# A hybrid decoder layer on one core: a new cost table for the order of the queues, an alternating first merge, attention blocks in twos

## The chip, the core and the metric

The kernel runs on one core of one Trainium2 chip. The core has a matrix engine (TensorE, PE in the profile; PEld is its loading of weights), a vector engine (VectorE, DVE), a scalar engine (ScalarE, ACT), a general engine (GpSimd, POOL) and a queue that issues transfers (SyncE, SP). Each engine works through its own instructions in the order in which the program holds them. The metric is the time of one execution in microseconds (us), as the median of several.

## The reference

One decoder layer in float32 on 1024 tokens of width 1024:

```
x = x + 0.5 * SwiGLU_1(rmsnorm(x))                 # 1024 -> 2816 -> 1024
h = rmsnorm(x);  columns = h @ w_in                # one projection for both branches
A: causal dilated window attention, 3 groups (dilations 1, 4, 16), 4 heads of 64 each, blocks of 128
B: gated DeltaNet, 8 heads of 128, chunks of 64, a triangular solve in each chunk
x = x + (sigmoid(g_a) * (A @ w_branch_a) + sigmoid(g_b) * (B @ w_branch_b)) @ w_out
x = x + 0.5 * SwiGLU_2(rmsnorm(x));  return rmsnorm(x)
```

## The kernel before

The program is one straight line: first feed-forward, mixer, merge of the branches, second feed-forward. Every large product is made of three float32r matmuls of 128 x 128 weights on 128 x 512 columns (high part, low part, cross part); `proj`, line 161, is the one of the mixer. They are called wide below.

Between them stand narrow matmuls in float32. `attention_pair` (lines 847 to 896) takes two heads of a group at a time and, for each of eight query blocks of 128, makes the scores of the two heads with 64 rows of weights each, one head in rows 0 to 63 of the array and one in rows 64 to 127 (L864, into two banks `tC`), masks them and takes the maximum on DVE (L867, L869), takes the exponential on ACT (L871), transposes on PE (L877, into `tM`), copies on DVE (L879), multiplies by the values on PE (L885, into `tA`), copies on ACT (L887) and stores (L896). `combine` (L910 to L931) reads the three groups back and weighs them, token tile by token tile.

`gdn_merge` joins the inverses of 32 x 32 blocks that `gdn_inverse_blocks` (L1036 to L1042, a long row of small DVE operations) has made: first in two quadrants of 32 rows (L1070 and L1075, eight chunks each, and one copy a quadrant), then in halves of 64 (L1083, L1090). In L1070 both quadrants write into one PSUM bank, on partitions 32 to 63 and 96 to 127.

The order on the engines doesn't follow the code. The program is built twice: `arrange` takes the first build, gives each instruction a cost (`Program.cost`) and a rank (the longest chain of costs from it to the end), and lets each engine in turn take the ready instruction of the highest rank; the second build is held to that order. `Program.turn` adds what PE loses between two kinds of matmul: R is wide, T a transpose, F a full float32 one, S the scores (64 rows), Q the small ones of the merge. A rule keeps PE on the instruction that follows in the code if its rank is at most `STAY` behind. Nothing of this runs on the chip; only the order that comes out does.

Of the kernel before, what the change touches and what calls it, by code (L numbers as in the profile page):

```python
# [8 lines left out]
F32 = mybir.dt.float32  # L9
F32R = mybir.dt.float32r  # L10
I32 = mybir.dt.int32
AF = mybir.ActivationFunctionType
# [3 lines left out]
P = 128  # L16
# [830 lines left out]
def attention_pair(C, w_in, g, hp, V):  # L847

    nc = C.nc
    q = rope_tile(C, w_in, C_QA + g * 256 + hp * P, g)  # L850
    k = rope_tile(C, w_in, C_KA + g * 256 + hp * P, g)
    with band(C, "att"):
        for b in range(NT):
            prev = (g == 0 and b > 0) or (g == 1 and b % 2 == 1)
            nk = 256 if prev else P
            mask = C.pair if g == 2 else (C.band if prev else C.band[:, P:])
            nj = nk // P
            o = C.at.tile([P, 132], F32, name="o", tag="o", bufs=3)
            nm = C.at.tile([P, 2], F32, name="nm", tag="nm", bufs=3)
            s = C.at.tile([P, 2, 256], F32, name="s", tag="s", bufs=3)  # L860
            ps = [psum(C, "tC") for _ in range(2)]
            for h in range(2):
                rows = slice(h * 64, h * 64 + 64)
                nc.tensor.matmul(ps[h][:, :nk], seq_tokens(q, rows, b), seq_tokens(k, rows, b, prev),  # L864
                                 start=True, stop=True)
            for h in range(2):
                nc.vector.tensor_tensor_reduce(s[:, h, :nk], ps[h][:, :nk], mask, 1.0, NEG, op0=ALU.add, op1=ALU.max,  # L867
                                               accum_out=o[:, 128 + h:129 + h])
            nc.vector.tensor_scalar(nm, o[:, 128:130], -0.125, None, op0=ALU.mult)  # L869
            for h in range(2):  # L870
                nc.scalar.activation(s[:, h, :nk], s[:, h, :nk], AF.Exp, bias=nm[:, h:h + 1], scale=0.125,  # L871
                                     accum_out=o[:, 130 + h:131 + h])
            pt = psum(C, "tM")
            for h in range(2):
                for j in range(nj):
                    c = (h * nj + j) * P
                    nc.tensor.transpose(pt[:, c:c + P], s[:, h, j * P:j * P + P], C.ident)  # L877
            pT = C.at.tile([P, 512], F32, name="pT", tag="pT", bufs=2)
            nc.vector.tensor_copy(pT[:, :2 * nk], pt[:, :2 * nk])  # L879
            po = psum(C, "tA")  # L880
            for h in range(2):
                for j in range(nj):
                    vb = b - 1 + j if prev else b
                    c = hp * P + h * 64
                    nc.tensor.matmul(po[:, h * 64:h * 64 + 64], pT[:, (h * nj + j) * P:(h * nj + j) * P + P],  # L885
                                     V[vb][:, c:c + 64], start=j == 0, stop=j == nj - 1)
            nc.scalar.copy(o[:, :P], po[:, :P])  # L887
            dst = C.od[g][:, hp, :]
            if g == 0:
                dst = dst[b * P:b * P + P, :]  # L890
            elif g == 1:
                r, n = b // 2, b % 2
                dst = dst.rearrange("(i r) f -> r i f", r=4)[r, n * P:n * P + P, :]
            else:
                dst = dst.rearrange("(i r) f -> r i f", r=8)[b]
            nc.sync.dma_start(dst, o)  # L896


# [157 lines left out]
def gdn_merge(C, N, Tm, Um):  # L1056

    nc = C.nc

    def rows(ps, n):  # L1060
        return ps[:, :4 * n].rearrange("p (c t) -> p c t", t=n)

    half = (slice(0, 4), slice(4, 8))

    quads = [(slice(b, b + 32), slice(b + 32, b + 64)) for b in (0, 64)]
    ps = psum(C, "tM")
    W = C.gd.tile([P, NT, 32], F32, name="W", tag="W", bufs=2)
    for lo, hi in quads:
        for c in range(NT):
            nc.tensor.matmul(ps[hi, c * 32:c * 32 + 32], N[lo, c, hi], Tm[lo, c, lo], start=True, stop=True)  # L1070
        nc.vector.tensor_copy(W[hi], ps[hi, :256].rearrange("p (c t) -> p c t", t=32))
    ps = psum(C, "tM")
    for lo, hi in quads:
        for c in range(NT):
            nc.tensor.matmul(ps[hi, c * 32:c * 32 + 32], Um[hi, c, hi], W[hi, c, :], start=True, stop=True)  # L1075
# [442 lines left out]
class Program:  # L1518
# [118 lines left out]
    def form(self, i):  # L1637
        aps = [a for a in i["ins"] if a["kind"] == "physical_ap"]
        if i["engine"] == "PE":
            if aps[0]["dtype"] == "float32r":  # L1640
                return "R"
            if i.get("is_transpose"):
                return "T"
            return "F" if aps[0]["ap"][0][1] > 64 else "S" if i["outs"][0]["ap"][0][1] > 64 else "Q"
        if i["engine"] == "Activation":
            return {"Exp": "E", "Silu": "U", "Sigmoid": "G", "Ln": "L"}.get(str(i.get("func")).split(".")[-1], "")
        return ""

    def turn(self, a, b, n):

        if a == b:
            return 0
        if b == "S" or b == "Q" or a == "Q":
            return (200 if n < 256 else 300) if a == "S" else 93
        if a == "S":
            return 200 if n < 256 else 300
        return -80 if b == "R" and a in "TF" else 6

    def run(self, a):
        n = 1  # L1660
# [6 lines left out]
    def cost(self, k):  # L1667
# [13 lines left out]
            n *= c  # L1681
        q = self.queue[k]
        if q == 0:
            t = {"R": n / 2.4 + 13, "T": 109, "F": 223, "S": 7, "Q": 117 if n > 32 else 63}[self.kind[k]]
            return t, t + 190 + (300 if self.kind[k] == "S" else 0)
        ps = any(self.place[a["memref"]][0] == "PSUM" for a in aps)
        if q == 1:
            t = 150 + 1.04 * n
# [18 lines left out]
STAY = 1000  # L1707


def hop(a, b):  # L1710
# [3 lines left out]
def arrange(prog, pools):  # L1714
# [15 lines left out]
    while stack:  # L1730
        k = stack.pop()
        rank[k] = cost[k][1] if k < n else 0.0
        for c, whole in kids[k]:
            rank[k] = max(rank[k], rank[c] + (cost[k][1] + hop(p.queue[k], p.queue[c]) if whole else 0))
# [21 lines left out]
    while count < n:  # L1756
# [19 lines left out]
        k = now[q][0][1]  # L1776
        if q == 0 and last[0] is not None:
            f = follow.get(last[0])
            if f is not None and not taken[f] and not left[f] and ready[f] <= t and rank[f] >= rank[k] - STAY:
# [14 lines left out]
        clock[q] = t + cost[k][0]  # L1794
        if q == 0:
            free0 = clock[q]
            clock[q] -= 80 if p.kind[k] in "TF" else 0
        end = t + cost[k][1]
        if p.dma[k]:
            end += max(0.0, wire - clock[q] - 1500)  # L1800
# [67 lines left out]
```

## Time and profile before

| | |
|---|---|
| median of 3 runs | 2573.09 us (2571.34 to 2573.66) |
| the profiled execution, its own time | 2572.86 us |
| its span in the trace | 2571.1 us |
| time outside the span | 1.8 us |
| instructions | 34921 |

A row of the timeline has the start in us, the busy time in us, engine, line, operation, the tiles written and read, and how many equal ones were merged into it. A float32 matmul that is no transpose runs as two passes and has two records: x16 at L1070 is eight matmuls. A row of the stages has the length of the stretch, the busy time of each engine with its instructions, the share of the TensorE clock that was granted, and the DMA share. A matmul's record is longer than its turn on PE, so what one costs is read from start to start. A row of waits has the waiting group, what it waited for, us in all, times, and the longest.

### The profile page before, as it was taken

To read this page: it belongs to the slowest core of one execution; us is meant where nothing else is said; L and a number is where in the kernel's file an instruction comes from. 1 tells how busy PE (TensorE), PEld (TensorE's weight loads), DVE (VectorE), ACT (ScalarE), POOL (GpSimd) and SP (SyncE) were. 2 spreads that over 40 slices of the span, in tenths; PEclk is the share of its full clock that TensorE was granted. 3 is DMA by queue.
4 is the path that set the end of the run, shared out by engine and by line. 5 is a ranking of instruction groups with operands and counts; after the bars stand their busy time and mean duration, and the time that the engine had idled before them with its cause. 6 is when DMAs were issued, how large, how long until landed. Compare 5 with 4: busy or idle time off the path is not lost.

```text
span 2571.1 us, 34921 instructions
## 1 busy us (share of the span) xinstructions
PE 2508.9 (98%) x12739; PEld 2074.0 (81%) x12739; DVE 1825.5 (71%) x4059; ACT 983.8 (38%) x1899; POOL 24.4 (1%) x36
## 2 busy tenths in 40 slices
PE   7999999999999999899999999989999999999996
PEld 7788888888888877688888888868888888888885
DVE  8867666768744455888888888546668766667578
ACT  4422332444422336333443335254443333333443
POOL 0000000000000000000000000000000000000000
PEclk9999999999999999999999999999999999999998
DMA  4233224836343331322222213255542223328453
GB/s 159 80 115 114 99 96 168 289 109 203 118 123 94 93 82 52 91 66 64 56 62 56 68 48 81 66 184 193 182 137 91 106 91 115 115 98 301 138 168 111
DMA packets 258172, 301.06 MB, mean 117 GB/s; under 512 B 41840, under 2 KB 175184, under 8 KB 258000
## 3 DMA queue, kind: packets, MB, share of 16 engines
q1 hardware_dynamic: 255696, 292.54, 34.8%
q10 hardware_dynamic: 2304, 6.29, 1.0%
q8 instruction: 100, 1.64, 0.3%
q14 instruction: 72, 0.59, 0.1%
HBM read 217.34 MB, written 75.14 MB: 114 GB/s over the span
## 4 chain that ended last, share of the span: by engine, by line
PE 90%; DVE 6%; DMA 2%; ACT 1%; issue 1%; SPq 0%; DVEq 0%; ACTq 0%
PE mm L161 22%; PE tC L404 13%; PE mm L404 8%; PE tM L404 8%; PE mm L584 4%; PE tC L584 4%; PE tA L161 3%; PE tM L584 3%; PE tA L584 3%; PE mm L697 2%; PE mm L274 2%; PE tC L274 2%; PE tC L1381 2%; PE mm L1381 2%; DMA sgl<-sgbd 1%; PE tA L885 1%
## 5 line engine op out<-in xcount | busy, mean ns | idle before, releaser
L216 ACT CAST fH<-fraw 128x512 fp32r<-128x512 f32 x482 | 289.1, 620 | 463.6 <-PE tM L404 89.4
L217 DVE TENSOR_TENSOR fL<-fraw,fH 128x512 fp32r<-128x512 f32 x482 | 323.0, 689 | 123.8 <-ACT fH L216 118.9
L161 PE MATMUL mm<-hH,fH 128*128 128x512 f32 x896 | 361.5, 410 | 8.7 <-ACT xp L955 5.0
L161 PE MATMUL mm<-hH,fL 128*128 128x512 f32 x896 | 361.0, 405 | 0.0
L161 PE MATMUL mm<-hL,fH 128*128 128x512 f32 x896 | 360.3, 404 | 0.0
L161 PEld LDWEIGHTS mm<-hH,fH 128*128 128x128 f32 x896 | 169.9, 190 | 43.4 <-ACT xp L955 6.2
L161 PEld LDWEIGHTS mm<-hH,fL 128*128 128x128 f32 x896 | 169.7, 190 | 33.3 <-issue 2.3
L161 PEld LDWEIGHTS mm<-hL,fH 128*128 128x128 f32 x896 | 170.1, 190 | 30.3 <-issue 1.7
L404 PE MATMUL mm<-hL,fH 128*128 128x512 f32 x320 | 124.5, 389 | 0.0
L404 PE MATMUL mm<-hH,fL 128*128 128x512 f32 x320 | 121.2, 389 | 0.1
L404 PE MATMUL mm<-hH,fH 128*128 128x512 f32 x320 | 119.0, 389 | 0.0
L576 ACT CAST fH<-hid 128x512 fp32r<-128x512 f32 x154 | 95.0, 617 | 53.1 <-DMA hid<-hd1x 15.8
L577 DVE TENSOR_TENSOR hid<-hid,fH 128x512 fp32r<-128x512 f32 x154 | 104.5, 685 | 5.5 <-ACT fH L576 5.5
L438 DVE TENSOR_TENSOR e<-tM,e 128x512 f32<-128x512 f32 x40 | 26.1, 687 | 79.0 <-PE tM L404 79.0
L216 ACT CAST fH<-hH 128x512 fp32r<-128x512 f32 x68 | 42.3, 622 | 91.3 <-PE tC L584 33.3
L867 DVE CUSTOM_DVE_ANT_0 s<-tC,masks 128x128 f32<-128x128 f32 (+1 forms) x96 | 30.4, 350 | 58.4 <-PE tC L864 35.1
L404 PEld LDWEIGHTS mm<-hH,fL 128*128 128x128 f32 x320 | 60.1, 188 | 13.0 <-DVE fL L217 0.5
L965 DVE SCALAR_TENSOR_TENSOR ka<-xp,cw,ka 128x512 f32<-128x512 f32 x96 | 69.4, 757 | 1.3 <-ACT ka L963 0.8
L404 PEld LDWEIGHTS mm<-hH,fH 128*128 128x128 f32 x320 | 60.0, 188 | 12.6 <-ACT e L408 0.2
L404 PEld LDWEIGHTS mm<-hL,fH 128*128 128x128 f32 x320 | 60.1, 188 | 12.4
L584 PE MATMUL tC<-fH 128*128 128x512 f32 x176 | 68.4, 390 | 0.0
L584 PE MATMUL tC<-fL,fH 128*128 128x512 f32 x176 | 68.2, 389 | 0.0
(402 smaller groups left out, 6200.4 us busy)
## 6 DMA issues: line engine op xcount, KB each, us to landing
fraw<-in_w_in_dram SPq DMA_DIRECT2D x66, 512.0 KB, 3.8
fraw<-in_ffn_w_gate_dram SPq DMA_DIRECT2D x22, 1024.0 KB, 5.2
fraw<-in_ffn_w_up_dram SPq DMA_DIRECT2D x22, 1024.0 KB, 7.2
hL<-in_ffn_w_down_dram SPq DMA_DIRECT2D x8, 1024.0 KB, 6.3
fraw<-in_ffn_w_down_dram SPq DMA_DIRECT2D x8, 1024.0 KB, 6.1
fraw<-in_w_branch_b_dram SPq DMA_DIRECT2D x8, 1024.0 KB, 5.6
fraw<-in_w_out_dram SPq DMA_DIRECT2D x8, 1024.0 KB, 7.3
vb<-xp ACTq DMA_DIRECT2D x48, 128.0 KB, 2.4
```

The costliest lines, as they stand in the source:

```text
L161: nc.tensor.matmul(ps, w, x, start=k == 0 and i == 0, stop=k == kt - 1 and i == 2)
L216: nc.scalar.copy(h, src)
L217: nc.vector.tensor_tensor(out=l, in0=src, in1=h.bitcast(F32), op=ALU.subtract)
L274: nc.tensor.matmul(ps[:, n0:n0 + n], w, x[:, k, c], start=k == 0 and i == 0, stop=k == KT - 1 and i == 2)
L404: nc.tensor.matmul(ps, w, x, start=opens and k == 0 and q == 0, stop=k == 3 and q == 2, skip_group_check=True)
L576: C.nc.scalar.copy(h, v.bitcast(F32))
L577: C.nc.vector.tensor_tensor(out=v, in0=v.bitcast(F32), in1=h.bitcast(F32), op=ALU.subtract)
L584: self.C.nc.tensor.matmul(ps, x[:, m], w, start=p == 0 and i == 0, stop=p == NPAIR - 1 and i == 2)
L697: nc.tensor.matmul(ps[:, :n], h[:, k, b * P:b * P + P], W[k][w], start=k == 0 and i == 0, stop=k == KT - 1 and i == 2)
L867: nc.vector.tensor_tensor_reduce(s[:, h, :nk], ps[h][:, :nk], mask, 1.0, NEG, op0=ALU.add, op1=ALU.max, accum_out=o[:, 128 + h:129 + h])
L965: nc.vector.scalar_tensor_tensor(o, x, w, o, op0=ALU.mult, op1=ALU.add)
L1381: nc.tensor.matmul(ps, mx[:, c], W[k][w], start=i == 0, stop=i == len(seq) - 1)
```

## The change

Three things are edited.

`attention_pair` handles query blocks b and b + 1 together. Their four score matmuls are written in one piece (head 0 and head 1 of the first block, then of the second), into the two halves of the same two `tC` banks; one operation scales the four maxima, one ACT copy takes both results out of `tA` and one transfer stores them: 24 of each in place of 48. The transposes, the copies of `pT` and the products with the values stay one for each block. The tiles `o`, `nm` and `s` are twice as large with two buffers in place of three.

`gdn_merge` issues its first two stages with the chunk as the outer loop, so that the two quadrants alternate, and copies both quadrants after all sixteen.

The table of `arrange` is new. PE's turns have other prices, and the two heads' scores are told apart as S and s; scores cost 106 + 0.83 ns a column. DVE and ACT are free for the next instruction 82 and 100 ns before the end of one, and an instruction that needs the result of the one just before on the same engine comes 40 ns after its end. While PE is on narrow matmuls it prefers a ready narrow one of a rank at most `LINGER` = 3000 behind; while on wide ones, a wide one at most `STAY` = 1000 behind.

```diff
-        for b in range(NT):
+        for b0 in range(0, NT, 2):
...
+            for i, (b, prev, nj, _) in enumerate(blocks):
+                for h in range(2):
+                    rows = slice(h * 64, h * 64 + 64)
+                    nc.tensor.matmul(ps[h][:, i * 256:i * 256 + nj * P], seq_tokens(q, rows, b), seq_tokens(k, rows, b, prev),
+                                     start=True, stop=True)
...
+            nc.scalar.copy(o[:, :, :P], po[:, :256].rearrange("p (b f) -> p b f", f=P))
...
+    for c in range(NT):
+        for lo, hi in quads:
+            nc.tensor.matmul(ps[hi, c * 32:c * 32 + 32], N[lo, c, hi], Tm[lo, c, lo], start=True, stop=True)
     for lo, hi in quads:
-        for c in range(NT):
-            nc.tensor.matmul(ps[hi, c * 32:c * 32 + 32], N[lo, c, hi], Tm[lo, c, lo], start=True, stop=True)
         nc.vector.tensor_copy(W[hi], ps[hi, :256].rearrange("p (c t) -> p c t", t=32))
...
-        if a == b:
+        if a == b or a + b == "Ss":
             return 0
...
+        t = (205 if n < 256 else 305) if a == "S" else 260 if b == "s" else 0
+        if b in "SsQ":
+            return t + (0 if a in "Ss" else 93)
...
-        return t, t
+        return t - (0, 82, 100, 0)[q], t
...
+            wide = p.kind[last[0]] == "R"
...
+            if f is not None and rank[f] >= rank[k] - (STAY if wide else LINGER):
                 k = f
...
-                at = clock[q]
+                at = end + 40 if q in (1, 2) else clock[q]
```

The instructions are the same 11692 matmuls; their order differs nearly everywhere. Counted over the whole order of PE, in unbroken stretches of one kind:

| stretches | before | changed |
|---|---|---|
| scores, of one / two / four matmuls | 16 / 40 / 0 | 2 / 9 / 19 |
| small ones of the merge (32 and 64 wide) | 76 | 56 |
| wide followed by a transpose or a full float32 one | 380 | 259 |
| neighbours in the 32-wide merge that lie in different rows of the array | 15 | 230 |

PE late in the attention, before (`s` are the exponentials, `ka` holds keys, queries or values):

```order
L885 MATMUL tA<-ka,pT 128x64 x2
L161 MATMUL mm<-hH_5387,fH 128x512
L161 MATMUL mm<-hL_5389,fH 128x512
L161 MATMUL mm<-hH_5387,fL 128x512
L864 MATMUL tC<-ka 128x128
L161 MATMUL mm<-hL_5719,fH 128x512
L161 MATMUL mm<-hH_5717,fL 128x512
L864 MATMUL tC<-ka 128x128
```

And in the changed program, where the lines of the same operations are 883, 866 and 890:

```order
L890 MATMUL tA<-ka,pT 128x64 x2
L883 MATMUL tM<-ident,s 128x128 x2
L890 MATMUL tA<-ka,pT 128x64 x2
L883 MATMUL tM<-ident,s 128x128 x2
L866 MATMUL tC<-ka 128x128 x4
L890 MATMUL tA<-ka,pT 128x64 x4
L161 MATMUL mm<-hH_5387,fH 128x512
```

Narrow matmuls stand together and the four scores of two blocks follow each other, where two heads of one block stood with wide ones between them.

PE at the first merge of head 0, before (`Tm`, `U` are the inverse and its transpose, `W` the first product):

```order
L1070 MATMUL tM<-Tm,ka 32x32 x4
L1075 MATMUL tM<-W,U 32x32 x8
L1070 MATMUL tM<-Tm,ka 32x32 x4
L161 MATMUL mm<-hH_5388,fL 128x512
L161 MATMUL mm<-hH_5388,fH 128x512
L161 MATMUL mm<-hL_5390,fH 128x512
L161 MATMUL mm<-hH_5388,fL 128x512
L1004 MATMUL tA<-seg,strictR 128x512 x2
L161 MATMUL mm<-hL_5720,fH 128x512
L161 MATMUL mm<-hH_5718,fL 128x512
L1075 MATMUL tM<-W,U 32x32 x4
```

And changed:

```order
L1074 MATMUL tM<-Tm,ka 32x32 x16
L161 MATMUL mm<-hH_5717,fH 128x512
L161 MATMUL mm<-hL_5719,fH 128x512
L161 MATMUL mm<-hH_5717,fL 128x512
L1080 MATMUL tM<-W,U 32x32
L161 MATMUL mm<-hH_5388,fL 128x512
L1080 MATMUL tM<-W,U 32x32 x15
```

The sixteen of a stage stand in one piece, and in it the two quadrants alternate.

DVE where `combine` (L910 to L925) meets the inverse of head 0 (L1036, L1037), before:

```order
L914 TENSOR_TENSOR cz<-ce,oc 128x12
L915 TENSOR_TENSOR cM<-cz 128x4
L916 TENSOR_TENSOR cM<-cM,cz 128x4
L917 RECIPROCAL cM<-cM 128x4
L918 TENSOR_TENSOR ce<-ce,cM 128x12
L922 TENSOR_TENSOR oc<-oc,ce 128x3x128 x2
L924 TENSOR_TENSOR cy<-oc 128x256
L925 TENSOR_TENSOR cy<-cy,oc 128x256
```

And changed (`combine` now at L914 to L929, the inverse at L1045 and L1046):

```order
L918 TENSOR_TENSOR cz<-ce,oc 128x12
L1045 TENSOR_TENSOR fsP<-fsT,Tm 128x80
L919 TENSOR_TENSOR cM<-cz 128x4
L217 TENSOR_TENSOR fL<-fraw,fH 128x512
L920 TENSOR_TENSOR cM<-cM,cz 128x4
L1046 TENSOR_REDUCE fsT<-fsP 128x4
L921 RECIPROCAL cM<-cM 128x4
L217 TENSOR_TENSOR fL<-fraw,fH 128x512
L1045 TENSOR_TENSOR fsP<-fsT,Tm 128x84
L922 TENSOR_TENSOR ce<-ce,cM 128x12
```

An instruction no longer stands right behind the one whose result it reads. From the first operation of `combine` to the first copy of the merge, DVE has 223 instructions before, of which 134 are read by their successor, and 252 in the changed program, of which 22 are; the 29 more are parts of head 1 (its convolutions, splits and sums). PE has 248 wide ones of `proj` from its last product of the attention to the first L1070 before, and 259 to the first L1074 in the changed program; the last product of the attention itself stands 72 wide ones earlier in the mixer.

More of the change, by code (lines that the diff above doesn't have):

```diff
@@ L852, in attention_pair @@
     with band(C, "att"):
-        for b in range(NT):
[L854 to L860, printed above, removed]
-            ps = [psum(C, "tC") for _ in range(2)]
[L862 to L879, printed above, removed]
-            po = psum(C, "tA")
[L881 to L887, printed above, removed]
@@ new lines, in attention_pair @@
+        for b0 in range(0, NT, 2):
+            blocks = []
+            for b in (b0, b0 + 1):
+                prev = (g == 0 and b > 0) or (g == 1 and b % 2 == 1)
+                mask = C.pair if g == 2 else (C.band if prev else C.band[:, P:])
+                blocks.append((b, prev, 2 if prev else 1, mask))
+            o = C.at.tile([P, 2, 132], F32, name="o", tag="o", bufs=2)
+            nm = C.at.tile([P, 2, 2], F32, name="nm", tag="nm", bufs=2)
+            s = C.at.tile([P, 2, 2, 256], F32, name="s", tag="s", bufs=2)
+            ps = [psum(C, "tC") for _ in range(2)]
+            for i, (b, prev, nj, _) in enumerate(blocks):
[3 more added lines that the diff above has]
+                                     start=True, stop=True)
+            for i, (b, prev, nj, mask) in enumerate(blocks):
+                for h in range(2):
+                    nc.vector.tensor_tensor_reduce(s[:, i, h, :nj * P], ps[h][:, i * 256:i * 256 + nj * P], mask, 1.0, NEG,
+                                                   op0=ALU.add, op1=ALU.max, accum_out=o[:, i, 128 + h:129 + h])
+            nc.vector.tensor_scalar(nm, o[:, :, 128:130], -0.125, None, op0=ALU.mult)
+            po = psum(C, "tA")
+            for i, (b, prev, nj, _) in enumerate(blocks):
+                for h in range(2):
+                    nc.scalar.activation(s[:, i, h, :nj * P], s[:, i, h, :nj * P], AF.Exp, bias=nm[:, i, h:h + 1], scale=0.125,
+                                         accum_out=o[:, i, 130 + h:131 + h])
+            for i, (b, prev, nj, _) in enumerate(blocks):
+                pt = psum(C, "tM")
+                for h in range(2):
+                    for j in range(nj):
+                        c = (h * nj + j) * P
+                        nc.tensor.transpose(pt[:, c:c + P], s[:, i, h, j * P:j * P + P], C.ident)
+                pT = C.at.tile([P, 512], F32, name="pT", tag="pT", bufs=2)
+                nc.vector.tensor_copy(pT[:, :2 * nj * P], pt[:, :2 * nj * P])
+                for h in range(2):
+                    for j in range(nj):
+                        vb = b - 1 + j if prev else b
+                        c = hp * P + h * 64
+                        nc.tensor.matmul(po[:, i * P + h * 64:i * P + h * 64 + 64], pT[:, (h * nj + j) * P:(h * nj + j) * P + P],
+                                         V[vb][:, c:c + 64], start=j == 0, stop=j == nj - 1)
+            nc.scalar.copy(o[:, :, :P], po[:, :256].rearrange("p (b f) -> p b f", f=P))
@@ L1067, in gdn_merge @@
     W = C.gd.tile([P, NT, 32], F32, name="W", tag="W", bufs=2)
+    for c in range(NT):
+        for lo, hi in quads:
+            nc.tensor.matmul(ps[hi, c * 32:c * 32 + 32], N[lo, c, hi], Tm[lo, c, lo], start=True, stop=True)
     for lo, hi in quads:
-        for c in range(NT):
-            nc.tensor.matmul(ps[hi, c * 32:c * 32 + 32], N[lo, c, hi], Tm[lo, c, lo], start=True, stop=True)
         nc.vector.tensor_copy(W[hi], ps[hi, :256].rearrange("p (c t) -> p c t", t=32))
     ps = psum(C, "tM")
+    for c in range(NT):
+        for lo, hi in quads:
+            nc.tensor.matmul(ps[hi, c * 32:c * 32 + 32], Um[hi, c, hi], W[hi, c, :], start=True, stop=True)
     for lo, hi in quads:
-        for c in range(NT):
-            nc.tensor.matmul(ps[hi, c * 32:c * 32 + 32], Um[hi, c, hi], W[hi, c, :], start=True, stop=True)
         nc.vector.tensor_copy(Tm[hi, :, lo], ps[hi, :256].rearrange("p (c t) -> p c t", t=32))
@@ L1733, in arrange @@
         for c, whole in kids[k]:
-            rank[k] = max(rank[k], rank[c] + (cost[k][1] + hop(p.queue[k], p.queue[c]) if whole else 0))
+            if whole:
+                near = p.queue[k] == p.queue[c] and not p.dma[k]
+                step = cost[k][1] + (hop(p.queue[k], p.queue[c]) if not near else 40 if p.queue[k] in (1, 2) else 0)
+                rank[k] = max(rank[k], rank[c] + (cost[k][0] if near and not p.queue[k] else step))
+            else:
+                rank[k] = max(rank[k], rank[c])
         for d in list(full[k]) + list(after[k]):
@@ L1778, in arrange @@
             f = follow.get(last[0])
-            if f is not None and not taken[f] and not left[f] and ready[f] <= t and rank[f] >= rank[k] - STAY:
+            wide = p.kind[last[0]] == "R"
+            if f is None or taken[f] or left[f] or ready[f] > t:
+                f = None
+            if f is None or (p.kind[f] == "R") != wide:
+                alike = [(r, c) for r, c in now[0] if not taken[c] and (p.kind[c] == "R") == wide]
+                f = min(alike)[1] if alike else f
+            if f is not None and rank[f] >= rank[k] - (STAY if wide else LINGER):
                 k = f
```

23 lines of the change are left out of this document (10 added, 13 removed).

## The prediction

> **What bounds the kernel now.** I read the page first, then the stages, then what PE waited for, then the timeline where PE changes its kind of work.
>
> ```profile
> span 2571.1 us, 34921 instructions
> PE 2508.9 (98%) x12739; PEld 2074.0 (81%) x12739; DVE 1825.5 (71%) x4059; ACT 983.8 (38%) x1899; POOL 24.4 (1%) x36
> PE 90%; DVE 6%; DMA 2%; ACT 1%; issue 1%; SPq 0%; DVEq 0%; ACTq 0%
> ```
>
> PE has work in flight for 98% of the span and is 90% of the chain that ended last. So most of what PE is spared comes off the time, and the question is what it is spared. Three stages of the mixer:
>
> ```profile
> 740.00:1030.00 290.00, 290.00 (x1694) 234.81 (x1694) 140.88 (x382) 115.34 (x343) 2.89 (x4) 1.00 0.30 84
> 1030.00:1108.00 78.00, 67.77 (x328) 53.85 (x326) 67.43 (x225) 27.81 (x54) 0.57 (x2) 0.93 0.36 97
> 1108.00:1690.00 582.00, 580.01 (x3567) 479.41 (x3567) 475.43 (x1354) 227.22 (x447) 19.75 (x26) 1.00 0.23 65
> ```
>
> Attention (first row) and heads 1 to 7 (third) never let PE run dry, while DVE is busy 141 of 290 us and 475 of 582. Between them, where `combine` and head 0 meet, PE is busy 67.8 of 78 us, DVE 67.4, and the clock falls to 0.93. What PE waits for there:
>
> ```profile
> PE mm L161 <- ACT xp L955: 5.0, 2, 4.9
> PE tA L928 <- DVE cM L916: 2.6, 1, 2.6
> PE tA L928 <- DVE cy L925: 2.4, 2, 2.1
> ```
>
> ```profile
> 1074.71 0.79 PE L161 MATMUL mm<-hH,fH 128*128 128x512 f32 x1 [4.86 <-ACT xp L955]
> 1075.30 0.63 PE L161 MATMUL mm<-hL,fH 128*128 128x512 f32 x1
> 1075.73 0.63 PE L161 MATMUL mm<-hH,fL 128*128 128x512 f32 x1
> ...
> 1079.11 0.39 PE L161 MATMUL mm<-hL,fH 128*128 128x512 f32 x1
> 1079.34 0.40 PE L161 MATMUL mm<-hH,fL 128*128 128x512 f32 x1
> ```
>
> A wide matmul takes 0.23 us from start to start (1079.11 to 1079.34) and 0.43 after the wait (1075.30 to 1075.73). From 1074.71 to 1079.11 that costs 2.2 us over ten wide ones at 0.23. With the waits (2.6, 2.1 and 4.9) this place loses about 12 us.
>
> **The change, part by part.**
>
> *Turns of PE, scores.*
>
> ```profile
> 1017.75 0.40 PE L161 MATMUL mm<-hH,fH 128*128 128x512 f32 x1
> 1018.07 0.48 PE L864 MATMUL tC<-ka 64*128 64x128 f32 x2
> 1018.49 0.50 PE L161 MATMUL mm<-hH,fL 128*128 128x512 f32 x1
> 1018.83 0.40 PE L161 MATMUL mm<-hH,fH 128*128 128x512 f32 x1
> ...
> 1020.84 0.40 PE L161 MATMUL mm<-hH,fH 128*128 128x512 f32 x1
> 1021.17 0.49 PE L864 MATMUL tC<-ka 64*128 64x128 f32 x4
> 1021.59 0.50 PE L161 MATMUL mm<-hL,fH 128*128 128x512 f32 x1
> 1021.93 0.27 PE L877 MATMUL tM<-ident,s 128*128 128x128 f32 x1
> 1021.96 0.48 PE L161 MATMUL mm<-hL,fH 128*128 128x512 f32 x1
> 1022.27 0.40 PE L161 MATMUL mm<-hH,fL 128*128 128x512 f32 x1
> ```
>
> Two heads' scores in one piece stand 0.42 us (1021.17 to 1021.59), and one head's alone stands 0.42 too (1018.07 to 1018.49). With the two wide ones around it, the one takes 1.09 us (1020.84 to 1021.93) and the other 1.08 (1017.75 to 1018.83), 0.63 and 0.62 over two wide ones. Hence a turn into scores and back costs 0.63 - 0.42 = 0.21, and a pair torn apart 2 x 0.62 - 0.63 = 0.61 more. Before, 8 of the 48 pairs are torn (16 stretches of one); of the change, one is: 7 x 0.61 = 4.3 us. The other 47 pairs stand in 28 stretches, 19 of which hold two pairs; each of those saves one turn, 19 x 0.21 = 4.0. The first pair of such a stretch goes on into the second head to head, which no row shows; if that costs a full turn, the 4.0 is nothing. The rows nearest to it are those of two heads in one piece, so I take it whole. Sum 8.3, bounds 4.3 and 8.3 (wider score tiles would only raise it).
>
> *Turns of PE, merge.*
>
> ```profile
> 1105.64 0.49 PE L1154 MATMUL tA<-ident,vT 128*128 128x128 f32 x3
> 1106.07 0.69 PE L1070 MATMUL tM<-Tm,ka 32*32 32x32 f32 x16
> 1106.68 0.73 PE L1004 MATMUL tA<-seg,strictR 128*128 128x512 f32 x2
> 1107.25 0.27 PE L1154 MATMUL tA<-ident,vT 128*128 128x128 f32 x1
> ...
> 1108.30 0.21 PE L1075 MATMUL tM<-W,U 32*32 32x32 f32 x1
> 1108.33 0.19 PE L1070 MATMUL tM<-Tm,ka 32*32 32x32 f32 x1
> 1108.36 0.19 PE L1075 MATMUL tM<-W,U 32*32 32x32 f32 x1
> ...
> 1108.42 0.48 PE L1075 MATMUL tM<-W,U 32*32 32x32 f32 x10
> 1108.71 0.21 PE L1070 MATMUL tM<-Tm,ka 32*32 32x32 f32 x1
> ```
>
> From 1108.42 to 1108.71 nine or ten passes start in one quadrant: 0.032 us each, 0.063 for a matmul of two passes. The stretch of eight from 1105.64 to 1107.25 takes 1.61 us; without three transposes at 0.11 (below) and two wide ones, 0.82; the eight at 0.063 are 0.51, so a turn costs 0.31. The change has 56 stretches of these in place of 76: 20 x 0.31 = 6.2 us.
>
> *Turns, transposes and full float32.* A transpose and the wide one after it take 0.34 us (1021.93 to 1022.27), so a transpose costs 0.11, which is about its own work: these turns are worth some 0.01. 121 fewer of them are 1.2 us. Turns together: 8.3 + 6.2 + 1.2 = 15.7, at least 11.7.
>
> *The alternating merge.* Between 1108.30 and 1108.36 a pass of one quadrant and one of the other start every 0.03 us, each quadrant at its own pace: two run at once. They overlap for about four matmuls at each change. With 230 neighbours of 240 in different quadrants, a matmul comes every 0.032 in place of 0.063: 230 x 0.031 = 7.1 us, less the 15 changes at 0.09 that exist, 1.4: 5.7 us. But there the two quadrants write different banks (L1070 and L1075 each have their own `tM`), and in the change they write the same one. No row shows this; the bounds are 5.7 and, if they take turns at 0.063, a loss of the 1.4. I take 5.7, since they lie on different partitions, as in the overlapping rows. That both copies now come after sixteen adds at most 8 x 0.063 = 0.5 us to a chain, which wide work hides.
>
> The Trainium skill speaks against this term: "TensorEngine Tiling (Array Packing)", Restrictions and Gotchas, says that different row tiles cannot access the same PSUM bank at the same time. By it the term would be a loss of 1.4 us and the time 7.1 us longer than mine.
>
> *DVE at `combine`.*
>
> ```profile
> 1034.19 0.17 DVE L918 TENSOR_TENSOR ce<-ce,cM 128x12 f32<-128x12 f32 x1
> 1034.28 0.68 DVE L979 TENSOR_REDUCE gssq<-sq 128x4 f32<-128x512 f32 x1
> ...
> 1036.73 0.17 DVE L125 TENSOR_SCALAR rgy<-rgv 128x16 int32<-128x16 int32 x1
> 1036.94 0.17 DVE L126 CUSTOM_DVE_ANT_0 rgy<-rgy,magic 128x32 uint16<-128x32 uint16 x1
> ```
>
> A small operation that the next one reads holds DVE 0.21 us (1036.73 to 1036.94); one that the next doesn't read 0.09 (1034.19 to 1034.28). The order has 134 - 22 = 112 fewer such neighbours between `combine` and the merge: 112 x 0.12 = 13 us of DVE. It spends them on 29 operations of head 1 there; at 0.45 us (an estimate between the 0.17 and the 0.68 of these rows, since both sizes are among them) that is 13 us too. So DVE needs the same time to the merge, but PE has 11 more wide ones to fill it (259 against 248), 2.5 us, and the wide ones that waited for `xp` depend on convolutions that now start earlier. The place loses 12 us; I take half, 6. Bounds: 0, if DVE still ends last, and 12.
>
> *Attention in twos and narrow work in a piece.* DVE is spared 24 scalings of 0.17 and ACT and SP 24 copies and stores, all hidden under PE in a stage where DVE is busy half the time. What it costs is cover: the product with the values waits for the copy of the transposes.
>
> ```profile
> 1024.62 0.39 PE L877 MATMUL tM<-ident,s 128*128 128x128 f32 x2
> ...
> 1025.04 0.42 DVE L879 COPY pT<-tM 128x256 f32<-128x256 f32 x1 [0.66 <-PE tM L877]
> ...
> 1025.76 0.55 PE L885 MATMUL tA<-ka,pT 128*128 128x64 f32 x4
> ```
>
> The last of the two transposes starts at 1024.73, the product at 1025.76: 1.03 us, about 1.3 for the wider copy. In the change the other block's narrow work stands between, at the tightest some 1.2 us of it, elsewhere 1.4 to 7. Where DVE is late with the copy, PE stands, and behind it the wide ones. I take a loss of 2 us for the 48 blocks, bounds 0 and 10 (0.2 at each).
>
> *The rest* (feed-forward, the start, the mixer's end where PE waits for data to come back, the last stores) keeps its instructions; PE or a transfer sets its pace, and I take nothing.
>
> Sum: -15.7 - 5.7 - 6 + 2 = -25.4. From the profiled execution's 2572.86 us (0.2 below the median of the runs): 2547.5.
>
> **The rivals.** *One bank, one quadrant at a time*: as above, 2547.5 + 5.7 + 1.4 = 2554.6. For it: the bank is shared; against it: the partitions differ. *The wait at `combine` stays*: DVE sets the pace there, and the 2 us of turns saved in front of it become waiting too: 2547.5 + 6 + 2 = 2555.5. For it: DVE does as much as before; against it: the attention ends 72 wide ones (16 us) earlier in the order, so that DVE starts on it earlier. *The wait closes*: if no wait is as long as the 4.9 us that the slow stretch follows, the clock may stay up, and the other 6 us go as well: 2541.5. For it: 112 fewer waits of DVE for itself; against it: that time is already filled with head 1. *Slower*: the narrow stretches are in order on PE, so each late copy or exponential holds the wide work that could have run; three such places for each of 24 pairs of blocks. At 0.5 us each they take 36 us: 2547.5 - 2 + 36 = 2581.5. It decides from 0.38 us a place on (27.4 / 72). For it: the cover at the tightest is below the 1.3 us of the wide copy; against it: most places have twice that.
>
> **How the numbers follow.** Forecast 0.50 (2540 to 2554 by itself), shared bank 0.15, the wait stays 0.17, the wait closes 0.11, slower 0.07. The range for 8 in 10 takes the full 12 us and no loss at the low end (2572.9 - 15.7 - 5.7 - 12 = 2539.5, and 4 for the start and the tail, where DVE has chains of its own: 2535) and at the high end the smallest turns, nothing from the merge and the wait, and some loss of cover (2572.9 - 11.7 + 1.4 + 2 = 2564.6): 2535 to 2565. A measurement of this kernel tells about 0.2% (5 us) from no change; faster than that 0.86, within it 0.07 (the wait stays and the cover fails a little), slower 0.07.
>
> **What would show it.** Scores: a stretch of four at 0.84 us, not 1.05. Merge: sixteen of L1074 in 0.5 us, not 1.0. `combine`: PE's waits there at about 6 us. Attention: PE busy all the time and shorter, with no waits for `pT`. I am wrong if the attention shows waits of PE for DVE of more than 10 us in all, or if the waits between 1000 and 1080 us grow.

## The result and the profile after

The changed kernel takes 2555.65 us (median of four), the kernel before 2573.38 beside it: 0.9929 of its time, interval 0.991 to 0.9949. One of the four executions took 11541.96 us; the ratio leaves it out, and the median of the other three, 2554.51 us, stands for the change where runs below are compared with it. That is 0.7% faster with an interval clear of 1, inside the range, and 7 to 8 us more than the forecast of 2547.5. It lies just outside the 2540 to 2554 that the forecast had for itself.

The page of the changed kernel: span, engines, and the chain that ended last.

```profile
span 2552.8 us, 34782 instructions
PE 2490.4 (98%) x12739; PEld 2070.5 (81%) x12739; DVE 1766.6 (69%) x4035; ACT 974.1 (38%) x1875; POOL 24.6 (1%) x36
PE 86%; DVE 9%; DMA 2%; ACT 1%; issue 1%; SPq 0%; DVEq 0%; ACTq 0%
```

To see where the 18.3 us of span went, both executions are cut at the same seven pieces of work: first matmul to first attention score; to the last product of the attention; to the first merge matmul; to the last matmul of the scans; to the merge of the branches; to the last matmul; to the end. Columns: stretch, its length, busy time of PE, PEld, DVE, ACT and POOL with their instructions, granted clock, DMA share, GB/s. The kernel before:

```profile
9.50:749.40 739.90, 730.19 (x3428) 611.46 (x3428) 533.77 (x977) 276.93 (x487) 0.96 (x1) 1.00 0.41 140
749.40:1025.90 276.50, 276.50 (x1621) 223.36 (x1621) 134.44 (x374) 109.82 (x331) 0.96 (x1) 1.00 0.29 80
1025.90:1106.10 80.20, 69.97 (x329) 55.83 (x328) 67.27 (x224) 30.36 (x59) 2.51 (x4) 0.94 0.37 101
1106.10:1700.80 594.70, 592.11 (x3642) 489.27 (x3642) 482.81 (x1378) 231.90 (x455) 19.75 (x26) 1.00 0.23 64
1700.80:1772.80 72.00, 61.70 (x266) 50.41 (x265) 34.99 (x56) 37.49 (x62) 0.00 (x0) 0.93 0.59 201
1772.80:2551.00 778.20, 778.01 (x3460) 643.60 (x3461) 553.30 (x979) 289.79 (x495) 0.00 (x0) 1.00 0.41 141
2551.00:2571.10 20.10, 0.39 (x2) 0.00 (x0) 15.62 (x61) 3.45 (x6) 0.00 (x0) 0.56 0.37 143
```

The changed kernel:

```profile
10.00:743.80 733.80, 726.73 (x3428) 611.52 (x3428) 519.50 (x971) 272.52 (x488) 0.95 (x1) 1.00 0.41 140
743.80:991.30 247.50, 247.50 (x1549) 210.65 (x1549) 119.67 (x341) 94.26 (x294) 1.53 (x2) 1.00 0.31 86
991.30:1078.50 87.20, 79.91 (x376) 62.98 (x376) 75.38 (x257) 51.78 (x85) 3.29 (x5) 0.94 0.38 102
1078.50:1686.70 608.20, 595.38 (x3667) 491.48 (x3666) 453.69 (x1353) 224.64 (x441) 18.60 (x24) 1.00 0.22 63
1686.70:1763.40 76.70, 66.17 (x283) 53.46 (x282) 40.19 (x64) 39.39 (x67) 0.00 (x0) 0.93 0.61 205
1763.40:2539.00 775.60, 774.32 (x3445) 640.32 (x3443) 544.73 (x992) 286.07 (x495) 0.00 (x0) 1.00 0.41 141
2539.00:2552.80 13.80, 0.34 (x2) 0.00 (x0) 9.60 (x39) 1.15 (x2) 0.00 (x0) 0.63 0.34 133
```

The lengths of single stretches can't be compared, since wide matmuls moved from one to another (1621 matmuls in the attention, now 1549). What can be compared is PE's busy time summed up to the last matmul (called its work below), the time in which PE was dry there (length less busy), and the tail behind the last matmul:

| us | PE's work | PE dry | tail |
|---|---|---|---|
| before | 2508.5 | 33.0 | 20.1 |
| changed | 2490.0 | 39.0 | 13.8 |

PE has 18.5 us less to do, stands dry for 6.0 more, and the tail is 6.3 shorter; with a first matmul 0.5 later that is the 18.3. The dry time fell from 9.7 to 7.1 before the attention and from 10.2 to 7.3 at `combine`, and rose from 2.6 to 12.8 in the merges and scans. A caution on the first column: a record of PE is longer than its turn, so a wait shorter than that lies hidden in it, and so does a slow clock.

The slow clock is not small here. Of the 18.5 us, 3.5 lie before the attention, where both kernels have the same 3428 records (730.19 and 726.73). The 50 us there, before and then changed:

```profile
690.00:740.00 50.00, 46.31 (x221) 38.91 (x220) 22.35 (x44) 14.11 (x26) 0.96 (x1) 0.93 0.49 137
690.00:740.00 50.00, 47.73 (x233) 40.17 (x232) 18.89 (x40) 12.52 (x24) 0.95 (x1) 1.00 0.47 128
```

Before, PE waits 3.7 us for `xp` (L828) and its clock is at half from 717 to 724 us; in the changed kernel the wait is 2.3 us and the clock stays at 1.00. So 15.0 us of the 18.5 are left for the turns and the merge.

What the prediction said would be seen, PE's timeline of the changed kernel at the first merge and at one score stretch:

```profile
1078.18 0.39 PE L161 MATMUL mm<-hL,fH 128*128 128x512 f32 x1
1078.49 0.69 PE L1074 MATMUL tM<-Tm,ka 32*32 32x32 f32 x32
1079.12 0.50 PE L161 MATMUL mm<-hH,fH 128*128 128x512 f32 x1
```

```profile
941.93 0.72 PE L866 MATMUL tC<-ka 64*128 64x128 f32 x8
942.58 0.66 PE L883 MATMUL tM<-ident,s 128*128 128x128 f32 x4
```

Sixteen merge matmuls (32 passes) take 0.63 us with the turn, where eight took 0.82 with both turns. They all write one bank, on different partitions. The Trainium skill's rule that different row tiles cannot access the same PSUM bank at once ("TensorEngine Tiling (Array Packing)", Restrictions and Gotchas) doesn't hold for these quadrants: by it sixteen matmuls at 0.063 would take 1.0 us. Four scores of 128 columns take 0.65 us, not the 0.84 of the forecast; one pair alone stood 0.42, so a second pair behind the first costs 0.23. Not all stretches are of this size: those with a second block of 256 columns take 0.85 us, and those with two such blocks 1.06, where one pair of 256 columns alone takes 0.63.

### The profile page after: what moved, and what is told of

Read it like the earlier page. It is cut to its first block, busy times and chain, and to the rows that moved or that the text cites. A ratio compares the mean times of both kernels' runs of the same rounds, so it can differ in the third digit from the quotient of the medians.

```text
span 2552.8 us, 34782 instructions
## 1 busy us (share of the span) xinstructions
PE 2490.4 (98%) x12739; PEld 2070.5 (81%) x12739; DVE 1766.6 (69%) x4035; ACT 974.1 (38%) x1875; POOL 24.6 (1%) x36
## 4 chain that ended last, share of the span: by engine, by line
PE 86%; DVE 9%; DMA 2%; ACT 1%; issue 1%; SPq 0%; DVEq 0%; ACTq 0%
PE mm L161 19%; PE tC L404 13%; PE mm L404 9%; PE tM L404 8%; PE mm L584 5%; PE tC L584 4%; PE tM L584 4%; PE tA L584 4%; PE tA L161 3%; PE mm L697 2%; PE mm L274 2%; PE tC L274 2%; PE mm L1387 2%; PE tC L1387 1%; PE tC L161 1%; PE tA L890 1%
## 5 line engine op out<-in xcount | busy, mean ns | idle before, releaser
L161 PE MATMUL mm<-hL,fH 128*128 128x512 f32 x896 | 356.0, 398 | 0.0
L404 PE MATMUL mm<-hL,fH 128*128 128x512 f32 x320 | 122.6, 389 | 0.0
L431 DVE TENSOR_TENSOR e<-tC,e 128x512 f32<-128x512 f32 x40 | 27.3, 686 | 66.9 <-PE tC L404 66.9
L584 PE MATMUL mm<-fL,fH 128*128 128x512 f32 x176 | 68.4, 390 | 0.0
```

The lines of the kernel that those rows point to most:

```text
L161: nc.tensor.matmul(ps, w, x, start=k == 0 and i == 0, stop=k == kt - 1 and i == 2)
L404: nc.tensor.matmul(ps, w, x, start=opens and k == 0 and q == 0, stop=k == 3 and q == 2, skip_group_check=True)
L431: tt(out=p1[i], in0=ps, in1=p1[i], op=ALU.add)
L584: self.C.nc.tensor.matmul(ps, x[:, m], w, start=p == 0 and i == 0, stop=p == NPAIR - 1 and i == 2)
```

## Experiments

The same cut was made in each run. All are timed against the kernel before; the last three columns are from each one's profiled execution, in us.

| kernel | median us | ratio and interval | PE's work | dry | tail |
|---|---|---|---|---|---|
| alternating merge alone | 2573.32 | 1.0001 [0.9992, 1.001] | 2505.0 | 36.0 | 20.1 |
| attention in twos alone | 2585.38 | 1.0047 [1.0034, 1.0059] | 2504.5 | 46.9 | 20.5 |
| table alone | 2557.99 | 0.9939 [0.9926, 0.9953] | 2503.6 | 30.3 | 13.7 |
| change, merge matmul priced 32 ns | 2546.7 | 0.9895 [0.9882, 0.9909] | 2490.3 | 30.8 | 14.0 |
| change, weaker wish to stay narrow | 2563.84 | 0.9965 [0.9952, 0.9977] | 2499.5 | 39.9 | 13.9 |
| change, dependent rule alone undone | 2654.92 | 1.0318 [1.0304, 1.0332] | 2529.3 | 100.0 | 13.5 |
| priced 32 ns, attention as before | 2553.09 | 0.9926 [0.9913, 0.9938] | 2496.0 | 31.1 | 13.7 |
| old table at 32 ns, alternating merge | 2571.69 | 0.9995 [0.9986, 1.0004] | 2505.0 | 34.6 | 20.1 |
| change, old vector prices | 2575.65 | 1.001 [1.0001, 1.0019] | 2494.0 | 47.6 | 17.1 |
| before, new vector prices | 2573.73 | 1.0004 [0.9995, 1.0013] | 2511.4 | 38.8 | 13.9 |
| change, merge and scores repriced | 2545.31 | 0.9891 [0.9877, 0.9904] | 2486.7 | 33.2 | 14.0 |
| the same, stronger wish to stay | 2547.91 | 0.9905 [0.9891, 0.9918] | 2489.8 | 35.5 | 13.7 |

### One part alone

*The alternating merge in the kernel before.*

```diff
+    for c in range(NT):
+        for lo, hi in quads:
+            nc.tensor.matmul(ps[hi, c * 32:c * 32 + 32], N[lo, c, hi], Tm[lo, c, lo], start=True, stop=True)
     for lo, hi in quads:
-        for c in range(NT):
-            nc.tensor.matmul(ps[hi, c * 32:c * 32 + 32], N[lo, c, hi], Tm[lo, c, lo], start=True, stop=True)
```

> The kernel before with the alternating merge alone; the table of before. Theory (two quadrants run at once even in one bank, and PE's spared time comes off): 210 of 240 neighbours alternate where 15 did, 195 x 0.031 = 6.0 us, less four more stretches of merge at 0.31: -4.8 us, 2568.5. Rival (PE only comes earlier to the copy that it has to wait for, since the table still holds a matmul for 0.063): the spared time turns up as waits of PE for DVE at the second stage of the merge, and the time stays at 2572 to 2574.

No change, as the rival said. PE's work is 3.5 us less and its dry time 3.0 more (3.7 more in the merges and scans): what the quadrants save is waited out.

*Attention in twos in the kernel before*, with the old table (its edit is that of `attention_pair` in the change).

> The kernel before with the attention in twos alone; the table of before. Theory (turns): 29 stretches of scores in place of 56, 19 of them with four matmuls, which in the changed kernel start 0.11 us apart from the second on: 7 torn pairs less at 0.61, 19 x some 0.4, five more stretches of merge at 0.31: about -10 us, 2563. The attention then ends some 10 us earlier and the wait at combine keeps its 12 us. Rival (pairs of blocks make longer chains, which PE waits for): waits of PE in the attention, 2570 or more.

12 us slower than the kernel before, where I had expected 10 less. PE's work falls by 4.0 us and its dry time rises by 13.9, 6.8 of it at `combine` and 5.4 in the merges and scans. The largest wait is the one that the kernel before has too, at `combine`, where the wide ones wait for `xp` for 12.8 us in place of 5.0. Waits of PE between 1030 and 1107 us in this run:

```profile
PE mm L161 <- ACT xp L959: 12.8, 2, 6.8
PE tA L932 <- DVE cy L929: 4.1, 2, 2.1
```

In the attention itself PE is dry for 0.7 us: this is not the slow rival of the prediction. Most of the loss lies behind the attention.

*The table in the kernel before* (its edit is that of `Program` and `arrange`).

> The kernel before with the new table alone. Theory (the table brings the shorter tail and the entry without a slow clock, -6 and -3 us, and 15 fewer stretches of merge, 8 pairs no longer torn, -9 us, but also the new waits in heads 1 to 7, +9): about -9 us, 2564, with 14 us from the last matmul to the end in place of 20. Rival (the tail comes from elsewhere, and the table brings only turns and waits): 2572, tail 20 us.

15.6 us less than the kernel before, where I had expected 9, with all 48 pairs of scores whole but none doubled. Of the span's 13.5, 4.8 is PE's work (2.3 of it before the attention, on the same matmuls), 2.8 dry time and 6.4 the tail (and 0.5 lost at the first matmul). Nearly two thirds of what the table gives is thus not PE's work but waits and the tail.

### Why the merge gained nothing

*The changed kernel with the right price.*

```diff
-"Q": 117 if n > 32 else 63}[self.kind[k]]
+"Q": 117 if n > 32 else 32}[self.kind[k]]
```

> The changed kernel with one price of the table altered: a 32-wide matmul of the merge holds PE for 32 ns, as the trace of the changed kernel has it when quadrants alternate, in place of 63. Theory (PE comes to the copies of the merge earlier than the table thinks, and waits): PE's waits for DVE at the merge's later stages (6.7 us in the changed kernel between 1090 and 1690 us) fall below 3, and the time by 4 us, to 2551.5. Rival (those waits come from DVE's own order or from narrow work being kept together): they stay at 6 us or more, 2554 to 2557.

8 us less than the change, twice what I expected, and the program on the chip has the same operations on each engine. PE's work is the same (2490.3 against 2490.0); the dry time is 8.2 less, 6.4 of it in the merges and scans. That stretch in this run, and below it PE's waits in it, first of the changed kernel and then of this one:

```profile
1080.50:1680.50 600.00, 593.62 (x3653) 489.86 (x3653) 448.00 (x1349) 223.85 (x441) 19.20 (x24) 1.00 0.23 64
```

```profile
PE tM L1096 <- DVE W L1091: 3.4, 6, 0.8
PE tM L1089 <- DVE Tm L1082: 1.9, 4, 0.6
...
PE tM L1080 <- DVE W L1076: 1.4, 3, 0.8
```

```profile
PE tM L1096 <- DVE W L1091: 1.9, 5, 0.8
...
PE tM L1089 <- DVE Tm L1082: 0.5, 2, 0.3
PE tM L1080 <- DVE W L1076: 0.5, 1, 0.5
```

In the changed kernel the sixteen matmuls are over 0.5 us before the table thinks so. The order places the next stage of the merge, which needs a copy by DVE, as if the copy had that much longer; PE is there early and stands, and the wide ones behind it stand too. The price changes nothing but the order, so this wait is shown to be one of the order. The three rows fall by 3.8 us together; the other 2.6 of the 6.4 are spread over smaller waits.

*The same price in the old table*, with the alternating merge and nothing else.

```diff
-"Q": 117 if n > 32 else 63, ...
+"Q": 117 if n > 32 else 32, ...
```

> The kernel before with its old table, the alternating merge, and that table's price for the merge's 32-column matmul set to 32 ns in place of 63 (the alternating merge alone, at the old price, took 2573.3 us). Theory A, the gain of alternating was lost because the table kept the slots of 63 ns and the PE waited them out: with the right price the 5.7 us of the prediction appear, 2567 to 2568 us. Theory B, the old table loses it for other reasons (single turns of the PE, the vector engine as the bound of the merge): 2573 us again.

2571.69 us, 1.6 less than at the old price, with intervals that overlap: no gain that can be told. PE's work is as before (2505.0), the dry time 34.6 against 36.0. A right price of one item is worth 8 us in the new table and next to nothing in the old one. What else the old table lacks for it isn't separated here; the next two runs show how much hangs on its vector prices.

### Turns of PE against prices of the vector engines

*The changed kernel without its vector prices.*

```diff
-        return t - (0, 82, 100, 0)[q], t
+        return t, t
...
-                step = cost[k][1] + (hop(...) if not near else 40 if p.queue[k] in (1, 2) else 0)
+                step = cost[k][1] + (hop(...) if not near else 0)
...
-                at = end + 40 if q in (1, 2) else clock[q]
+                at = clock[q]
```

> The changed kernel with all that the change did to the prices of VectorE and ScalarE undone: their issue time is again as long as the result takes, and a dependent instruction of the same engine may follow at the issue time, as in the kernel before; the turns, prices and preference of the PE are those of the change. (Undoing the second half of it alone took 2654.9 us, 99 us more than the change.) Theory A, the table's worth is in the turns of the PE, and the new vector prices only keep each other right: 2555 us, at most 3 us off. Theory B, the vector prices carry a part of the gain, since the tail and the start became shorter by some 12 us together, which no turn of the PE explains: 2564 to 2568 us, with a tail of about 20 us behind the last matmul.

Nothing of the gain is left, although PE's order has the same few stretches (26 of scores, 56 of merge matmuls, 295 wide ones; the change has 30, 56 and 299) and its work is 14.5 us below that of the kernel before. It stands dry for 14.6 us more: 17.0 in place of 10.2 at `combine`, most of it in one wait, and 10.7 in place of 2.6 in the merges and scans. The second theory is the nearer one; the loss is larger than it said, and the tail, 17.1 us, goes back only half of the way to 20. The first row is from PE's waits between 993 and 1077 us, the second is the tail:

```profile
PE tA L932 <- DVE cy L929: 10.2, 1, 10.2
```

```profile
2551.20:2568.30 17.10, 0.41 (x2) 0.00 (x0) 12.41 (x47) 2.30 (x4) 0.00 (x0) 0.66 0.40 154
```

The profiled execution took 2570.04 us, 5.6 less than the median, so the median's loss is larger than these numbers show. A rival is left: attention in twos, which this kernel has and which alone cost 12 us under the old table, with the same 17.0 us dry at `combine`. PE's half of the table was not run without it.

*The kernel before with only the vector prices.*

```diff
-        return t, t
+        return t - (0, 82, 100, 0)[q], t
...
-                at = clock[q]
+                at = end + 40 if q in (1, 2) else clock[q]
```

> The kernel before with nothing but the change's prices of VectorE and ScalarE (issue time 82 and 100 ns shorter than the result, a dependent instruction of the same engine 40 ns after the result), its PE prices and turns as before. Theory A of the run before (the turns are the worth): 2573 us, within 3. Theory B (the vector prices carry a part): 2561 to 2566 us, with a tail of about 14 us.

Again no gain as a whole: the first theory has the number. But the two ends move as the second has it. The first and the last stretch of this run:

```profile
10.00:744.00 734.00, 728.61 (x3430) 610.43 (x3430) 522.79 (x970) 276.97 (x487) 0.95 (x1) 1.00 0.42 140
...
2560.20:2574.10 13.90, 0.41 (x2) 0.00 (x0) 9.82 (x41) 2.09 (x4) 0.00 (x0) 0.65 0.34 132
```

The start is 5.9 us shorter (739.9 to 734.0) and the tail 6.2 (20.1 to 13.9): the vector prices alone are enough for both, though without them (the run above) the tail is 3.0 shorter too. Behind the last matmul DVE had 61 instructions left before, and has 41 here and 39 in the change; the others had been put earlier. Between the two ends this kernel loses what it won: dry 33.4 us against 23.3, and 4.5 more of work. So the vector prices are worth nothing alone, PE's half is worth nothing in the one kernel in which it was seen, and the whole table alone is worth 15.6 us.

*One rule of the vector prices undone.*

```diff
-                at = end + 40 if q in (1, 2) else clock[q]
+                at = clock[q]
```

> The changed kernel, with one rule of the order undone: an instruction of VectorE or ScalarE that reads what the same engine has just made may follow at the engine's issue time again, not 40 ns after the result is there. Theory A, the 6.3 us by which the work behind the last matmul became shorter (20.1 to 13.8 us) come from this rule, since it lets the order put other work between dependent vector instructions: the tail goes back to about 20 us and the time to 2562 us. Theory B, the tail is shorter because TensorE's own order brings the last norm's work earlier: the tail stays at 14 us and the time at 2555 to 2556 us.

I had asked only where the tail comes from; it stays at 13.5 us, so it isn't this rule by itself. But the kernel is 100 us slower than the change: 61 more of PE are dry (100.0 against 39.0), and its work is 39 more, at a granted clock of 0.983 over the span against 0.994. Of the dry time 52.3 us lie in this stretch (the row below it is the largest wait there):

```profile
1091.70:1772.70 681.00, 628.72 (x3713) 513.36 (x3713) 476.86 (x1357) 228.33 (x448) 19.06 (x24) 0.97 0.20 58
```

```profile
PE tC L1191 <- DVE S L1209: 20.6, 17, 4.3
```

With issue times shortened by 82 and 100 ns and nothing added for a dependent instruction, the table takes chains on DVE, such as the state `S` of the scans, to be faster than they are, and has PE ask for their results too early. The two numbers are one price: halved, it is worse than the old table by far.

### The rest of the table and a better version

*A weaker wish to stay among narrow work.*

```diff
-            if f is not None and rank[f] >= rank[k] - (STAY if wide else LINGER):
+            if f is not None and rank[f] >= rank[k] - STAY:
```

> The changed kernel, with the order's bound for staying inside narrow work set back to that of wide work (1000 in place of 3000), so that the turns and the prices are those of the change and only the wish to stay among transposes, scores and merge matmuls is weaker. The written order then has 323 wide stretches in place of 299, 63 merge stretches in place of 56 and 26 score stretches in place of 30. Theory A, fewer stretches are what the change is worth: three more narrow stretches at 0.2 to 0.3 us and 24 more wide ones at about 0.03 us give 1 to 2 us more, 2557 us. Theory B, staying too long is what makes the new short waits of TensorE on the merge's later stages (about 7 us in the trace of the change, none there before): these waits shrink to those of the kernel before, and the time falls to 2549 us.

9 us slower than the change, nearly all of it in PE's work (+9.5; dry +0.9). The first theory has the sign and is far too small: the order has 24 more wide stretches, 7 more of merge matmuls and 4 fewer of scores, and at 0.31, 0.21 and 0.03 these come to 2 us. The clock accounts for most of the rest: in this run it falls twice inside the merges and scans (to 0.90 and 0.93 in the rows of ten us from 1230, to 0.58 and 0.91 in those from 1390), 6.8 us of clock in all, while PE is busy for 9 to 10 us of each row. Neither the kernel before nor the change has such a row there. What brings it down isn't shown; PE waits 5.4 us for `Tm` (L1089 on L1082) in this stretch, against 1.9 in the change.

*The right price, attention one block at a time.* The edit is that of the price above, with `attention_pair` of the kernel before.

> The kernel before with the new table, the alternating merge and a price of 32 ns for the merge's 32-column matmul, but with the dilated attention one query block at a time as before; beside the same with query blocks in twos, which took 2546.7 us. Theory A, attention in twos is worth what its 19 double score stretches save on the PE, about 4 to 6 us: 2551 to 2553 us. Theory B, attention in twos costs waits behind the attention, as it did under the old table (12 us longer): this kernel is the faster one, 2541 us or less. Theory C, both cancel: 2546 to 2548 us.

2553.09 against 2546.7: with this table attention in twos is worth 6.4 us, of which 5.7 is PE's work. With the old table it cost 12.

*Scores repriced too.*

```diff
-"S": n * 0.83 + 106, "s": n * 0.83 + 106, "Q": 117 if n > 32 else 63
+"S": n * 0.81 + 7, "s": n * 0.81 + 7, "Q": 117 if n > 32 else 32
```

> The changed kernel with two prices set to what its trace shows: 32 ns for the merge's 32-column matmul (which alone took 2546.7 us) and 111 ns for a score matmul of 128 columns, 215 ns for one of 256 (two heads run at once). The attention is 27 score stretches of 0.2 to 0.8 us, priced up to 0.4 us too long each. If prices that are too long are waited out everywhere as in the merge: 3 to 8 us less, 2539 to 2544 us. If only where the PE has nothing else to do, which is in the merge and not in the attention: 2545 to 2548 us.

2545.31 us, 0.9891 of the kernel before: the fastest here, though only 1.4 us from the version with the merge's price alone, which is no more than these runs scatter. Prices too long cost little in the attention, where PE is never dry.

*And a preference of 6000 in place of 3000.*

```diff
-LINGER = 3000
+LINGER = 6000
```

> As the run before, with the preference for staying inside narrow work doubled (6000 in place of 3000; 1000 in place of 3000 took 2563.8 us beside 2555.7 us of the change). If the gain goes with the preference: 2 to 5 us less than that run. If 3000 has taken what there is (its written order has 290 wide stretches in place of 299 and as many narrow ones): within 2 us of it, or some us more as the short waits grow.

2547.91 us: 3000 had taken what there is.

## Where the prediction was right and where not

| step | forecast | measured |
|---|---|---|
| turns of PE and alternating merge | -15.7 - 5.7 = -21.4 | PE's work from the attention on -15.0 |
| wait at `combine` | -6 | dry -2.9, see below |
| cover in the attention | +2 | 0 (dry 0.0 in both) |
| the rest: start | 0 | PE's work -3.5 (clock), dry -2.6, first matmul +0.5 |
| the rest: merges and scans | 0 | dry +10.2 |
| the rest: mixer's end, second feed-forward | 0 | dry +0.2 and +1.1 |
| the rest: tail | 0 | -6.3 |
| sum | -25.4 | -18.3 |

**The turns** are the term that was mis-sized. By the steps before, table, alternation with its price, attention in twos, PE's work from the attention on falls by 2.6, 7.5 and 5.4 us (1778.3, 1775.7, 1768.2, 1762.8). The turns that I had put at 15.7 are the first and the last of these, 8.0: half as much. The alternating merge, put at 5.7, is the middle one, with the order that its price brings. These steps hold slow clock and short waits too, so a us or two of each is open. The doubled scores were undersized: I took a second pair to cost as much as the first, 0.42, and it costs 0.23. The oversized part is thus what the table alone should have saved, pairs no longer torn and fewer stretches, 11.7 by my sum; whether the turns were read too dear or came back as short waits isn't separated. That the change with the old vector prices has little work and yet no gain shows what the sum left out: it took turns saved on PE as time saved. They are only if the vector engines have their results ready in the shorter time, and what made them ready was, as far as these runs show it, the other half of the table, which I had priced at `combine` alone.

**The alternating merge** runs as forecast, two quadrants at a time in one bank, so the rival of the shared bank is wrong although its 2554.6 us lies next to the result. The step that failed is the next one, that all 5.7 come off the time: the table kept 63 ns for what takes 32, the merges and scans got 10.2 us of new waits (the table alone has 4.7 of them), and the right price took 6.4 away, 8 us in all. With it the kernel reaches 2546.7, where the forecast was 2547.5; that these agree is luck, since the start and the tail, put at nothing, give about as much as the turns, `combine` and the scans lack. I had read from a row of the old order that heads 1 to 7 "never let PE run dry", and carried that over to the new one.

**The wait at `combine`**: the long waits are gone, and short ones stand in their place. PE's waits of the changed kernel between 985 and 1110 us:

```profile
PE tA L979 <- ACT ka L970: 1.7, 2, 1.3
PE tA L1008 <- DVE seg L995: 1.5, 2, 1.3
PE tA L979 <- ACT Dm L1010: 1.1, 2, 0.8
PE tA L1135 <- DVE ka L1138: 1.0, 1, 1.0
...
PE tA L932 <- DVE cy L929: 0.9, 3, 0.4
```

And the clock: two stretches of ten us, of the kernel before and then of the changed one.

```profile
1060.00:1070.00 10.00, 5.11 (x23) 3.29 (x21) 9.10 (x39) 2.31 (x7) 0.00 (x0) 0.94 0.56 159
1070.00:1080.00 10.00, 5.29 (x14) 4.22 (x15) 9.51 (x25) 5.40 (x9) 0.00 (x0) 0.55 0.05 14
```

```profile
1060.00:1070.00 10.00, 5.99 (x24) 3.69 (x25) 9.72 (x21) 6.23 (x10) 1.27 (x2) 0.74 0.10 23
1070.00:1080.00 10.00, 9.63 (x73) 7.75 (x71) 8.55 (x19) 4.79 (x9) 0.75 (x1) 0.75 0.30 70
```

The slow stretch is as long as before (1.0 - 0.94 + 1.0 - 0.55 is 0.51 of ten us, and 0.26 + 0.25 is too): 10.2 us at half clock, from 1068.8 us on before and from 1064.8 in the change. Half of it used to fall on time in which PE stood anyway (PE busy for 5.0 of the 10.2); now more of it falls on work (7.7). So I had misread the 4.9 us wait that "the slow stretch follows": it starts behind the products at 1069.19, when the clock is already down. (The ten wide ones behind it cost 2.1 us, not 2.2.) DVE is busy for 9 us of every 10 in both, which is what I had said for the rival "the wait stays". So between nothing and 2.9 of the 6 came.

**Attention**: no wait for `pT`, as forecast, and the slow rival is out: it needed 27.4 us in 72 places and there is nothing. In the old table, though, attention in twos does cost 12 us, by a way that I had not listed: the waits come after the attention.

**The rest** was the largest omission beside the merge. I wrote that PE or a transfer sets the pace of start and tail. The tail is 15.6 us of DVE in 20.1 before, and the new vector prices shorten it by 6 (the run that has only these shows it). I had counted on chains of DVE there only for the low end of the range, with 4 us for both ends.

## What to carry to other kernels

A faster instruction can save nothing as long as the order doesn't know it: where a table sets the order, change the price with the code, and read from the waits just behind it whether the order asks too early. Issue time and result time of one engine are one price, to be changed together. Prices of different engines can be worth little apart and much together, as here: measure the whole table, then take parts away. Turns counted on the bound engine are no gain until the engines that feed it are shown to keep up. And busy time of PE is work only at an equal clock: compare the granted clock of a stretch before putting a difference down to turns.

## What the runs showed of the hardware

Two quadrants of 32 rows work at once even into one PSUM bank, on different partitions: 32 passes take 0.63 us with the turn, where 16 passes of one quadrant took 0.61 in the kernel before (1106.07 to 1106.68). Two heads of 64 rows and 128 columns run at once: one head's scores and two heads' both stand 0.42 us, and a second pair behind a first costs 0.23. And the slow stretch of PE's clock at `combine` is 10.2 us at half clock in both kernels. In the changed one no single wait there is above 1.3 us; before, one is 4.9, but it begins when the clock is already down. So it isn't one long wait that brings it; what does isn't shown.
